# Seven half-size products for eight over the first four k tiles of ten gate and up pairs

## The chip, the cores and the metric

The program runs on one core of one Trainium2 chip. Its time is the device time of one execution in microseconds. Several executions were timed and one was profiled; the profile gives the span of the program on the core and, for each engine, every instruction's start and length. The engines are named as in the profile: PE (TensorE's matmuls), PEld (TensorE's weight loads), DVE (VectorE), ACT (ScalarE), POOL (GpSimd) and SP (which issues the weight DMAs; SPq is its queue).

## The reference

A block of a hybrid decoder: three token mixers, then a gated feed-forward network. The change lies in the latter, whose shapes are 256 tokens, D_MODEL = 2048 and D_FF = 5632, all in float32:

```python
x = x + rms_norm(h, norm_mix_post[l])
h = rms_norm(x, norm_ffn_pre[l])
h = swiglu(h, ffn_w_gate[l], ffn_w_up[l], ffn_w_down[l])
x = x + rms_norm(h, norm_ffn_post[l])

def swiglu(h, w_gate, w_up, w_down):
    return (jax.nn.silu(h @ w_gate) * (h @ w_up)) @ w_down
```

## The kernel before

**Products.** A float32 product is made of three matmuls in TensorE's fp32r form. Each operand is held as a high part (rounded to fp32r) and a low part (the rest), and high times high, high times low and low times high are summed in PSUM. The activations are split once, into `xh` and `xl`, with the channel on the partition: 16 k tiles of 128 channels by 256 tokens. A matmul's stationary operand is one k tile of 128 tokens (t = 0 or 1), its moving operand 512 columns of weights, its result a PSUM tile of 128 tokens by 512 columns.

**Weights.** `weights` streams them from DRAM. SP loads 1 MB at a time into a tile `raw` (four k tiles by 512 columns; `raw_bufs` is 3). Each half of `raw`, two k tiles or 128x1024, is split: ACT copies it into `wh` (L214), DVE subtracts that from `raw` into `wl` (L216). `wh` and `wl` have three buffers each (`h_bufs` is 3), so a split can begin when the matmuls of the third split before it are done. Twelve matmuls use each split: two k tiles, two token halves, three matmuls (L262 to L264 in `block_a_steps`).

**Gate and up.** The loop over j in `build` makes eleven pairs of 512 gate columns and 512 up columns. For j = 0 the two blocks alternate every four k tiles; for the others all 16 k tiles of gate come first, then all 16 of up. That is 2 blocks x 16 k tiles x 2 halves x 3 = 192 matmuls and 16 splits for one pair. The gate block has two PSUM tiles of tag `mm` and the up block two of tag `ptg`; each tag has three buffers. When a gate block is done, ACT applies silu (L1150) into `g`; when an up block is done, DVE multiplies (L1154). Then `split_channels` transposes `g` on PE (L285, four transposes for each token half), and ACT and DVE split the result into `ah` and `al` (L287, L288) for the last product, `w_down`.

**Order.** A scheduler puts the instructions of each engine in one fixed order when the program is built; an engine then runs its own list from first to last, and one that waits holds up all behind it. The gate and up weights are cast, subtracted and multiplied in the same order on ACT, DVE and PE.

Of the kernel before, what the change touches and what calls it, by code (L numbers as in the profile page):

```python
# [8 lines left out]
F32 = mybir.dt.float32  # L9
F32R = mybir.dt.float32r  # L10
AF = mybir.ActivationFunctionType
ALU = mybir.AluOpType
AX = mybir.AxisListType

P = 128
T = 256
D = 2048
KD = D // P
# [122 lines left out]
class Builder:  # L141
# [45 lines left out]
        return self.cst_t[:, o:o + n]  # L187


    def weights(self, wp, src, kts, width):  # L190

        nc, tc = self.nc, self.tc
        g = 2048 // width
        for k0 in range(0, kts, g):
            gk = min(g, kts - k0)
            raw = wp.tile([P, 2048], F32, name=self.uid("raw"), tag="raw", bufs=self.raw_bufs)
            ahead = FIRST if self.feeds else self.ahead
            rv = raw[:, :gk * width].rearrange("p (k c) -> p k c", c=width)
            n = gk // 2 if self.feeds else gk
            for i in range(0, gk, n):  # L200
                with tc.high_priority(ahead):
                    with tc.issue_after(self.load) if self.feeds and self.load else contextlib.nullcontext():
                        self.load = nc.sync.dma_start(rv[:, i:i + n], src[k0 // g][:, i:i + n]).ins
                    if self.feeds:
                        self.feeds.pop(0)()
            hg = 1024 // width
            for h0 in range(0, gk, hg):
                hk = min(hg, gk - h0)
                wh = wp.tile([P, 1024], F32R, name=self.uid("wh"), tag="wh", bufs=self.h_bufs)
                wl = wp.tile([P, 1024], F32R, name=self.uid("wl"), tag="wl", bufs=self.h_bufs)  # L210
                n = hk * width
                s = raw[:, h0 * width:h0 * width + n]
                with tc.high_priority(ahead):
                    nc.scalar.copy(wh[:, :n], s)  # L214
                with tc.high_priority(ahead), tc.issue_after(self.hold) if self.hold else contextlib.nullcontext():
                    nc.vector.tensor_tensor(wl[:, :n], s, wh[:, :n].bitcast(F32), ALU.subtract)  # L216
                hv = wh.rearrange("p (k c) -> p k c", c=width)
                lv = wl.rearrange("p (k c) -> p k c", c=width)
                for k in range(hk):
                    yield k0 + h0 + k, hv[:, k], lv[:, k]  # L220
# [657 lines left out]
def build(tc, aps, out):  # L878
    nc = tc.nc
    b = Builder(tc)  # L880
# [5 lines left out]
    pp = b.pp = b.pool("pp", space=bass.MemoryType.PSUM)  # L886
    b.dp = b.pool("dram", space=bass.MemoryType.DRAM)
    cp = b.pool("const")
    wp = b.pool("wp")
# [3 lines left out]
    def acts(s):  # L893
        return (xp.tile([P, KD, T], F32R, name=f"{s}h", tag="xh"), xp.tile([P, KD, T], F32R, name=f"{s}l", tag="xl"))
# [6 lines left out]
    xh, xl = acts("x")  # L901
# [66 lines left out]
    def direct(o, lead):  # L968

        t = b.slab(lead)  # L970
        cols(o, lambda ps: b.scaled(t[:, :, lead:lead + T], ps))
        return t
# [11 lines left out]
    def stage(s):  # L984
        return sp.tile([P, 512], F32, name=b.uid(s), tag="stage", bufs=b.stage_bufs)
# [16 lines left out]
    for q in range(4):  # L1002
        s = [direct(o + q, 1) for o in (BLK_RK, BLK_R, BLK_RV)]
# [5 lines left out]
        s = [direct(o + q, 3) for o in (BLK_Q, BLK_K, BLK_V)]  # L1009
# [15 lines left out]
    split = {}  # L1025
# [60 lines left out]
    x1 = []  # L1086
# [32 lines left out]
    xh, xl = acts("h")  # L1119
# [7 lines left out]
    with tc.high_priority(None), tc.issue_after(last):  # L1127
        rs = []
# [13 lines left out]
    ap_ = b.pool("ap")  # L1142
    ah = ap_.tile([P, KF, T], F32R, name="ah")
    al = ap_.tile([P, KF, T], F32R, name="al")
    for j in range(FF // 512):
        g = [stage("silu") for _ in range(2)]

        def gate(ps, g=g):
            for t in range(2):
                nc.scalar.activation(g[t], ps[t], AF.Silu, scale=rs[t])  # L1150

        def up(ps, g=g):
            for t in range(2):
                nc.vector.scalar_tensor_tensor(g[t], ps[t], rs[t], g[t], ALU.mult, ALU.mult)  # L1154

        steps = [b.block_a_steps(wp, pp, aps[w][j], xh, xl, KD, f) for w, f in (("w_gate", gate), ("w_up", up))]
        if j == 0:
            for _ in range(0, KD, 4):
                for st in steps:
                    for _ in range(4):  # L1160
                        next(st)
        for st in steps:
            for _ in st:
                pass
        b.hold = None
        for t in range(2):
            b.split_channels(pp, g[t], ah, al, 4 * j, t)

    x1 = []
    for t in range(2):  # L1170
        x1.append(ap_.tile([P, D], F32, name=f"x1r{t}"))
        nc.gpsimd.dma_start(x1[t], x1d[t])
    n4 = full(xp, "n4", aps["n4"], tag="xl")
    od = xp.tile([P, 2, D], F32, name="od", tag="xh")
# [9 lines left out]
    for t in range(2):  # L1184
        o = [od[:, t, j * 512:(j + 1) * 512] for j in range(4)]
        x = [x1[t][:, j * 512:(j + 1) * 512] for j in range(4)]
# [30 lines left out]
```

## Time and profile before

| what | value |
|---|---|
| time, median of 3 runs (lowest, highest) | 1848.22 us (1847.03, 1849.6) |
| time of the profiled execution | 1846.92 us |
| span of the profiled execution | 1845.1 us |
| granted TensorE clock over the span, as a share of full speed | 0.996 |
| busy PE, DVE, ACT | 1827.5, 1123.7, 863.8 us |

The profiled execution took 1.8 us more than its span; that part lies around the program. The span is the kernel's own work, and a change in a stage shows there one for one if the stage lies on the chain that ends last. A matmul's row gives its length from start to modelled end, and matmuls overlap, so what a matmul costs PE is the distance between two starts. The same goes, by a little, for DVE and ACT.

### The profile page before, as it was taken

What the parts mean: (1) busy time and instruction counts of PE and PEld (TensorE: products, weight loads), DVE (VectorE), ACT (ScalarE), POOL (GpSimd) and SP (SyncE); (2) the same over time, 40 slices, a digit from 0 to 9 for tenths busy, and PEclk for the clock granted to TensorE, in tenths of its full rate; (3) what the DMA queues carried; (4) which work ended last, traced back from release to release, by engine and by line L of the source; (5) the groups of instructions that cost most, each with busy time, mean ns of one, the idle gap of its engine ahead of it and who ended that gap; (6) DMA issues with size and microseconds to landing.
All of it is one profiled execution on the core that took longest, in us unless ns stands there. A gap on an engine that the chain in (4) does not pass through costs nothing.

```text
span 1845.1 us, 27756 instructions
## 1 busy us (share of the span) xinstructions
PE 1827.5 (99%) x11516; PEld 1578.7 (86%) x11516; DVE 1123.7 (61%) x1652; ACT 863.8 (47%) x1089; POOL 41.0 (2%) x76
## 2 busy tenths in 40 slices
PE   9999999999999999999999999999999999999998
PEld 9999997999899988887788878888888888888886
DVE  6768567866786677746665556555545445444444
ACT  7545345534553465444444446444444444443443
POOL 0000000000100010000000000000000000000000
PEclk9999999999999999999999999999999999999999
DMA  7545445444544454657765556555555555555553
GB/s 263 176 168 183 146 148 189 168 159 138 183 170 159 144 181 161 221 179 271 279 218 185 186 202 231 197 187 185 195 191 183 187 196 187 207 203 185 202 185 136
DMA packets 58574, 347.45 MB, mean 188 GB/s; under 512 B 6480, under 2 KB 7760, under 8 KB 19920
## 3 DMA queue, kind: packets, MB, share of 16 engines
q1 hardware_dynamic: 50832, 328.23, 50.8%
q10 hardware_dynamic: 7328, 15.36, 2.3%
q8 instruction: 90, 1.47, 0.3%
q0 software_dynamic: 288, 2.10, 0.3%
q14 instruction: 36, 0.29, 0.0%
HBM read 330.98 MB, written 14.68 MB: 187 GB/s over the span
## 4 chain that ended last, share of the span: by engine, by line
PE 96%; DVE 1%; ACT 1%; DMA 1%; issue 0%; POOL 0%; ACTq 0%; POOLq 0%; DVEq 0%; SPq 0%
PE mm L263 21%; PE mm L264 21%; PE mm L262 21%; PE mm L242 8%; PE mm L241 8%; PE mm L243 8%; PE tp L285 1%; PE px L568 1%; PE pr L603 1%; PE pr L592 1%; PE psa L599 1%; DMA raw<-in_w_branch_dram 1%; PE pst L609 0%; PE px L753 0%; PE px L482 0%
## 5 line engine op out<-in xcount | busy, mean ns | idle before, releaser
L216 DVE TENSOR_TENSOR wl<-raw,wh 128x1024 fp32r<-128x1024 f32 x590 | 721.4, 1224 | 607.0 <-ACT wh L214 604.4
L214 ACT CAST wh<-raw 128x1024 fp32r<-128x1024 f32 x590 | 620.5, 1052 | 839.3 <-PE mm L264 601.8
L242 PE MATMUL mm<-xl,wh 128*128 128x256 f32 x1200 | 342.5, 286 | 1.6 <-DVE xl L915 1.5
L241 PE MATMUL mm<-xh,wh 128*128 128x256 f32 x1200 | 342.8, 286 | 0.1
L243 PE MATMUL mm<-xh,wl 128*128 128x256 f32 x1200 | 341.4, 285 | 0.0
L264 PE MATMUL mm<-wh,hl 128*128 128x512 f32 x704 | 274.7, 390 | 0.0
L263 PE MATMUL mm<-wl,hh 128*128 128x512 f32 x704 | 274.6, 390 | 0.0
L262 PE MATMUL mm<-wh,hh 128*128 128x512 f32 x704 | 250.9, 392 | 2.0 <-ACT hh L311 2.0
L242 PEld LDWEIGHTS mm<-xl,wh 128*128 128x128 f32 x1200 | 229.8, 191 | 3.6 <-DVE xl L915 2.2
L241 PEld LDWEIGHTS mm<-xh,wh 128*128 128x128 f32 x1200 | 229.8, 191 | 1.9 <-ACT xh L914 0.5
L243 PEld LDWEIGHTS mm<-xh,wl 128*128 128x128 f32 x1200 | 229.5, 191 | 0.9 <-issue 0.3
L262 PEld LDWEIGHTS mm<-wh,hh 128*128 128x128 f32 x704 | 132.4, 188 | 29.6 <-ACT hh L311 2.6
L263 PEld LDWEIGHTS mm<-wl,hh 128*128 128x128 f32 x704 | 132.5, 188 | 27.6 <-DVE wl L216 0.4
L264 PEld LDWEIGHTS mm<-wh,hl 128*128 128x128 f32 x704 | 132.4, 188 | 27.5
L263 PE MATMUL mm<-wl,xh 128*128 128x512 f32 x384 | 151.7, 395 | 0.3 <-DVE wl L216 0.3
L264 PE MATMUL mm<-wh,xl 128*128 128x512 f32 x384 | 150.6, 392 | 0.0
L262 PE MATMUL mm<-wh,xh 128*128 128x512 f32 x384 | 141.3, 392 | 0.0
L264 PE MATMUL mm<-wh,al 128*128 128x512 f32 x352 | 136.9, 389 | 0.0
L263 PE MATMUL mm<-wl,ah 128*128 128x512 f32 x352 | 136.9, 389 | 0.0
L262 PE MATMUL mm<-wh,ah 128*128 128x512 f32 x352 | 123.6, 389 | 0.0
L263 PEld LDWEIGHTS mm<-wl,xh 128*128 128x128 f32 x384 | 72.1, 188 | 16.9 <-issue 1.0
L262 PEld LDWEIGHTS mm<-wh,xh 128*128 128x128 f32 x384 | 72.1, 188 | 16.0 <-issue 1.3
(297 smaller groups left out, 1951.4 us busy)
## 6 DMA issues: line engine op xcount, KB each, us to landing
raw<-in_w_in_dram SPq DMA_DIRECT2D x72, 1024.0 KB, 4.9
raw<-in_w_mix_dram SPq DMA_DIRECT2D x48, 1024.0 KB, 5.0
raw<-in_w_gate_dram SPq DMA_DIRECT2D x44, 1024.0 KB, 4.8
raw<-in_w_up_dram SPq DMA_DIRECT2D x44, 1024.0 KB, 4.9
raw<-in_w_down_dram SPq DMA_DIRECT2D x44, 1024.0 KB, 4.9
raw<-in_w_branch_dram SPq DMA_DIRECT2D x24, 1024.0 KB, 4.9
raw<-in_w_out_dram SPq DMA_DIRECT2D x16, 1024.0 KB, 4.8
keep<-stage ACTq DMA_DIRECT2D x28, 256.0 KB, 4.4
```

The costliest lines, as they stand in the source:

```text
L214: nc.scalar.copy(wh[:, :n], s)
L216: nc.vector.tensor_tensor(wl[:, :n], s, wh[:, :n].bitcast(F32), ALU.subtract)
L241: nc.tensor.matmul(o, hs, xh[:, k], start=(k == 0 and c == 0), stop=False, skip_group_check=True)
L242: nc.tensor.matmul(o, hs, xl[:, k], start=False, stop=False, skip_group_check=True)
L243: nc.tensor.matmul(o, ls, xh[:, k], start=False, stop=(k == kts - 1), skip_group_check=True)
L262: nc.tensor.matmul(ps[t], xh[:, k, ts], h, start=(k == 0), stop=False)
L263: nc.tensor.matmul(ps[t], xh[:, k, ts], l, start=False, stop=False)
L264: return nc.tensor.matmul(ps[t], xl[:, k, ts], h, start=False, stop=(k == kts - 1))
L285: nc.tensor.transpose(ps[:, k], src[:, k * P:(k + 1) * P], self.cst("id"))
L568: nc.tensor.matmul(ps[h][:, n * P:(n + 1) * P], bkc[hs, c, n], arc[hs, c, n], start=True, stop=True)
L592: nc.tensor.matmul(pq[bb, us], st[u][:, n, bb], sav[:, n, us], start=not n, stop=True, skip_group_check=True)
L599: nc.tensor.matmul(ps[bb, us], X[bb, 2 * u + p], R[bb, us], start=True, stop=True)
```

## The change

Only the pairs j = 1 to 10 change, and in them the first four of the 16 k tiles. These four k tiles (two blocks of two), the two token halves, and the two matrices gate and up make a product of 2x2 blocks by 2x2 blocks: token half by k block, times k block by matrix. Eight block products are replaced by seven (Strassen's algorithm in Winograd's form), each with a contraction over two k tiles.

- `sums` runs once, after pair 0. It adds and subtracts blocks of the activations on DVE and splits the four sums into `S`.
- `gate_up` replaces the two calls of `block_a_steps`. It loads the first `raw` of gate and of up together, makes four differences of weight blocks on DVE into `T` (128x1024 each; t1 and t2 first, then t4 and t3), and splits each of seven operands just before its product: b11, t1, t2, b21, t3, b22, t4.
- `product` has six matmuls for a split (two k tiles, three matmuls, one token half's worth of rows), where `block_a_steps` has twelve.
- The products are summed in four PSUM tiles: X takes four products, Y, Z and W one each. ACT copies X three times and Y once into tiles `m` while they are being filled (`keep`). The last two copies of X are called u2 and u3, the first one m1, that of Y m5.
- The other 12 k tiles go on in the old way, into Z and X for gate and W and Y for up. At their end DVE adds the kept copies (L1225, L1230; u2 gets m5 at L1216) before silu and the product with up.
- `T` and `S` lie in the buffers that the x1 tiles get after the loop.

```diff
+    def gate_up(j, S, g):
+        raw = []
+        for w in ("w_gate", "w_up"):
+            r = wp.tile([P, 2048], F32, name=b.uid("raw"), tag="raw", bufs=b.raw_bufs)
+            nc.sync.dma_start(r.rearrange("p (k c) -> p k c", c=512), aps[w][j][0])
+            raw.append([r[:, 0:1024], r[:, 1024:2048]])
+        (b11, b21), (b12, b22) = raw
...
+        def product(ps, a, w, start):
+            h, l = b.split(wp, w)
+            for k in range(2):
+                nc.tensor.matmul(ps, a[0][:, k], h[:, k], start=start and k == 0, stop=False, skip_group_check=True)
+                nc.tensor.matmul(ps, a[0][:, k], l[:, k], start=False, stop=False, skip_group_check=True)
+                nc.tensor.matmul(ps, a[1][:, k], h[:, k], start=False, stop=k == 1, skip_group_check=True)
...
+        product(X, act(0, 0), b11, True)
+        m1 = keep(X)
+        t1 = sub(0, b12, b11)
+        product(Y, s_(0), t1, True)
+        m5 = keep(Y)
+        t2 = sub(1, b22, t1)
+        product(X, s_(1), t2, False)
+        u2 = keep(X)
+        product(Z, act(0, 1), b21, True)
+        t4 = sub(0, b21, t2)
+        t3 = sub(1, b22, b12)
+        product(X, s_(2), t3, False)
+        u3 = keep(X)
+        product(W, s_(3), b22, True)
+        product(X, act(1, 1), t4, False)
+        nc.vector.tensor_tensor(u2, u2, m5, ALU.add)
+        for w, ps in (("w_gate", (Z, X)), ("w_up", (W, Y))):
+            for k, h, l in b.weights(wp, aps[w][j], KD, 512, first=4):
...
+            if w == "w_gate":
+                nc.vector.tensor_tensor(m1, Z, m1, ALU.add)
+                for t, src in ((1, X), (0, m1)):
+                    nc.scalar.activation(g[t], src, AF.Silu, scale=rs[t])
+            else:
+                for ps_, m, t in ((W, u2, 0), (Y, u3, 1)):
+                    nc.vector.tensor_tensor(m, ps_, m, ALU.add)
+                    nc.vector.scalar_tensor_tensor(g[t], m, rs[t], g[t], ALU.mult, ALU.mult)
```

What this does to the order is shown at the border between pairs 1 and 2; the other borders have the same order. On DVE before, from the last two splits of pair 1 to the first of pair 2 (numbers are buffers; `silu` is g):

```order
L216 TENSOR_TENSOR wl_11697<-raw_11694,wh_11696 128x1024
L216 TENSOR_TENSOR wl_11713<-raw_11694,wh_11712 128x1024
L1154 SCALAR_TENSOR_TENSOR silu_11394<-mm_11536,rstd_11074,silu_11394 128x512
L1154 SCALAR_TENSOR_TENSOR silu_11395<-mm_11537,rstd_11086,silu_11395 128x512
L216 TENSOR_TENSOR wl_11731<-raw_11728,wh_11730 128x1024
L216 TENSOR_TENSOR wl_11747<-raw_11728,wh_11746 128x1024
L288 TENSOR_TENSOR al<-tp_11676,ah 128x4x128
L288 TENSOR_TENSOR al<-tp_11683,ah 128x4x128
L216 TENSOR_TENSOR wl_11765<-raw_11762,wh_11764 128x1024
```

On DVE with the change, from the split of t1 on; ahead of it stand t1, t2 and the split of b11, and behind the last row the splits of b22 and t4 (mm_11413 and mm_11412 are W and Y of pair 1, m_11450 and m_11474 its u2 and u3):

```order
L195 TENSOR_TENSOR wl_11747<-T_11728,wh_11746 128x1024
L1230 TENSOR_TENSOR m_11450<-mm_11413,m_11450 128x512
L1185 TENSOR_TENSOR T_11728<-raw_11724,T_11728 128x1024
L1230 TENSOR_TENSOR m_11474<-mm_11412,m_11474 128x512
L1231 SCALAR_TENSOR_TENSOR silu_11403<-m_11450,rstd_11074,silu_11403 128x512
L195 TENSOR_TENSOR wl_11760<-T_11728,wh_11759 128x1024
L1231 SCALAR_TENSOR_TENSOR silu_11404<-m_11474,rstd_11086,silu_11404 128x512
L195 TENSOR_TENSOR wl_11772<-raw_11724,wh_11771 128x1024
L1185 TENSOR_TENSOR T_11728<-raw_11726 128x1024
L296 TENSOR_TENSOR al<-tp_11708,ah 128x4x128
L1216 TENSOR_TENSOR m_11769<-m_11769,m_11756 128x512
L296 TENSOR_TENSOR al<-tp_11715,ah 128x4x128
```

Between the split of t1 and that of t3 there are now eleven instructions, among them the end of pair 1 (two additions, two products, two `al`), and each split of pair 2 stands behind part of that.

On PE with the change, in the same place, after the six matmuls of b11 and of t1 (mm_11729 is X, mm_11730 Z, mm_11732 W; wh_11759 belongs to t2, wh_11771 to b21, wh_11783 to t3, wh_11795 to b22):

```order
L1191 MATMUL mm_11729<-wh_11759,S 128x512
L293 MATMUL tp_11708<-cst_t,silu_11403 128x128 x4
L1191 MATMUL mm_11730<-wh_11771,hh 128x512
L1192 MATMUL mm_11729<-wl_11760,S 128x512
...
L1192 MATMUL mm_11729<-wl_11760,S 128x512
L1193 MATMUL mm_11729<-wh_11759,S 128x512
L293 MATMUL tp_11715<-cst_t,silu_11404 128x128 x4
L1192 MATMUL mm_11730<-wl_11772,hh 128x512
...
L1193 MATMUL mm_11730<-wh_11771,hl 128x512
L1191 MATMUL mm_11729<-wh_11783,S 128x512
L1191 MATMUL mm_11732<-wh_11795,S 128x512
L1192 MATMUL mm_11729<-wl_11784,S 128x512
```

The eight transposes of pair 1, which stood together ahead of pair 2's third matmul, now stand in two fours among the products of t2 and b21. A product's first matmul needs only the cast part, and is put ahead of the five that need the subtracted part. On ACT the order of that stretch is: cast of t2, copy m1, cast of b21, copy m5, cast for `ah`, copy u2, cast for `ah`, casts of t3, b22 and t4, cast of the next gate half, copy u3.

## Rows read from the trace of the kernel before

**Rows 1.** The page's part on busy time: span, then engines

```profile
span 1845.1 us, 27756 instructions
PE 1827.5 (99%) x11516; PEld 1578.7 (86%) x11516; DVE 1123.7 (61%) x1652; ACT 863.8 (47%) x1089; POOL 41.0 (2%) x76
```

**Rows 2.** The page's chain of work that ended last, by engine

```profile
PE 96%; DVE 1%; ACT 1%; DMA 1%; issue 0%; POOL 0%; ACTq 0%; POOLq 0%; DVEq 0%; SPq 0%
```

**Rows 3.** Window of one pair: length, busy time by engine, clock, DMA

```profile
core 0: us, PE busy (x) PEld busy (x) DVE busy (x) ACT busy (x) POOL busy (x), PEclk, DMA share, GB/s
1245.36:1289.80 44.44, 44.44 (x202) 36.89 (x201) 22.24 (x21) 19.22 (x20) 0.00 (x0) 1.00 0.54 190
```

**Rows 4.** The chain from 1100 to 1610 us: start, length, what

```profile
1245.36 0.87 PE tp L285 x8
```

**Rows 5.** Timeline, PE before the border of 1245 us: start, length

```profile
1244.51 0.39 PE L262 MATMUL mm<-wh,hh 128*128 128x512 f32 x1
1244.74 0.39 PE L263 MATMUL mm<-wl,hh 128*128 128x512 f32 x1
```

**Rows 6.** Timeline, DVE at that border (in brackets: idle before, releaser)

```profile
1239.00 1.23 DVE L216 TENSOR_TENSOR wl<-raw,wh 128x1024 fp32r<-128x1024 f32 x1 [1.50 <-ACT wh L214]
1240.14 1.40 DVE L1154 SCALAR_TENSOR_TENSOR silu<-mm,rstd,silu 128x512 f32<-128x512 f32 x2
...
1244.44 1.23 DVE L216 TENSOR_TENSOR wl<-raw,wh 128x1024 fp32r<-128x1024 f32 x1 [1.49 <-ACT wh L214]
1246.45 1.29 DVE L288 TENSOR_TENSOR al<-tp,ah 128x512 fp32r<-128x512 f32 x2 [0.79 <-ACT ah L287]
1248.05 1.23 DVE L216 TENSOR_TENSOR wl<-raw,wh 128x1024 fp32r<-128x1024 f32 x1 [0.31 <-ACT wh L214]
```

**Rows 7.** Timeline, ACT at that border

```profile
1243.35 1.05 ACT L214 CAST wh<-raw 128x1024 fp32r<-128x1024 f32 x1 [1.66 <-PE mm L264]
1245.83 1.07 ACT L287 CAST ah<-tp 128x512 fp32r<-128x512 f32 x2 [1.43 <-PE tp L285]
```

**Rows 8.** Groups by line and shape: count, busy us, mean ns, idle before

```profile
L1154 DVE SCALAR_TENSOR_TENSOR silu<-mm,rstd,silu 128x512 f32<-128x512 f32 x22 | 15.4, 743 | 0.0
L288 DVE TENSOR_TENSOR al<-tp,ah 128x512 fp32r<-128x512 f32 x22 | 14.2, 686 | 8.7 <-ACT ah L287 8.7
L924 DVE TENSOR_TENSOR x<-x,x 128x1024 f32<-128x1024 f32 x3 | 3.7, 1218 | 0.0
L556 ACT COPY bkt<-px 128x512 f32<-128x512 f32 x8 | 4.4, 590 | 3.6 <-PE px L555 3.6
```

**Rows 9.** Timeline, DVE: splits that run without a pause between them

```profile
869.92 2.35 DVE L216 TENSOR_TENSOR wl<-raw,wh 128x1024 fp32r<-128x1024 f32 x2
1104.77 3.49 DVE L216 TENSOR_TENSOR wl<-raw,wh 128x1024 fp32r<-128x1024 f32 x3
```

**Rows 10.** Timeline, PE after a wait for ACT

```profile
1099.51 0.73 PE L262 MATMUL mm<-wh,hh 128*128 128x512 f32 x2 [1.54 <-ACT hh L311]
```

**Rows 11.** Windows before the first pair (columns as in rows 3)

```profile
1098.00:1100.00 2.00, 0.49 (x2) 0.30 (x2) 1.38 (x4) 2.00 (x7) 0.54 (x1) 1.00 0.30 127
1100.00:1102.00 2.00, 1.03 (x6) 0.43 (x4) 1.95 (x3) 0.51 (x3) 0.01 (x1) 0.81 0.94 397
1102.00:1104.00 2.00, 1.34 (x3) 0.62 (x4) 2.00 (x8) 0.87 (x4) 0.00 (x0) 0.50 0.23 94
1107.00:1108.00 1.00, 1.00 (x4) 0.74 (x3) 1.00 (x2) 0.21 (x1) 0.00 (x0) 0.50 0.00 0
```

**Rows 12.** Timeline, PE in the last of these stretches

```profile
1107.07 0.63 PE L263 MATMUL mm<-wl,hh 128*128 128x512 f32 x1
1107.49 0.63 PE L264 MATMUL mm<-wh,hl 128*128 128x512 f32 x1
```

**Rows 13.** DMA queue's own waits from 1156 to 1600 us; the page's issues

```profile
SPq L203 <- DVE wl L216: 411.6, 80, 5.9
raw<-in_w_gate_dram SPq DMA_DIRECT2D x44, 1024.0 KB, 4.8
```

More of the change, by code (lines that the diff above doesn't have):

```diff
@@ L187, in cst, with split, weights @@
         return self.cst_t[:, o:o + n]
-    def weights(self, wp, src, kts, width):
+    def split(self, wp, s):
+        h = wp.tile([P, 1024], F32R, name=self.uid("wh"), tag="wh", bufs=self.h_bufs)
+        l = wp.tile([P, 1024], F32R, name=self.uid("wl"), tag="wl", bufs=self.h_bufs)
+        self.nc.scalar.copy(h, s)
+        self.nc.vector.tensor_tensor(l, s, h.bitcast(F32), ALU.subtract)
+        return h.rearrange("p (k c) -> p k c", c=512), l.rearrange("p (k c) -> p k c", c=512)
+    def weights(self, wp, src, kts, width, first=0):
         nc, tc = self.nc, self.tc
         g = 2048 // width
-        for k0 in range(0, kts, g):
+        for k0 in range(first, kts, g):
             gk = min(g, kts - k0)
@@ L1144, in build, with sums @@
     al = ap_.tile([P, KF, T], F32R, name="al")
+    def sums():
+        t = ap_.tile([P, 2, D // 2], F32, name="sums", tag="x1r0")
+        x = t[:, 0].rearrange("p (k t) -> p k t", k=4)
+        o = t[:, 1].rearrange("p (i k t) -> p i k t", i=4, k=2)
+        nc.vector.tensor_tensor(x, xh[:, 0:4].bitcast(F32), xl[:, 0:4].bitcast(F32), ALU.add)
+        a = [[x[:, 2 * c:2 * c + 2, r * P:(r + 1) * P] for c in range(2)] for r in range(2)]
+        for i, (p, q, op) in enumerate(((a[1][0], a[1][1], ALU.add), (o[:, 0], a[0][0], ALU.subtract),
+                                        (a[0][0], a[1][0], ALU.subtract), (a[0][1], o[:, 1], ALU.subtract))):
+            nc.vector.tensor_tensor(o[:, i], p, q, op)
+        sp_ = ap_.tile([P, 2, 4, 2, P], F32R, name="S", tag="x1r1")
+        nc.scalar.copy(sp_[:, 0], o)
+        nc.vector.tensor_tensor(sp_[:, 1], o, sp_[:, 0].bitcast(F32), ALU.subtract)
+        return sp_
@@ new lines, in gate_up, with act, sub, keep @@
+    def gate_up(j, S, g):
[5 more added lines that the diff above has]
+        (b11, b21), (b12, b22) = raw
+        T = ap_.tile([P, 2, 1024], F32, name=b.uid("T"), tag="x1r0")
+        X, Z = [pp.tile([P, 512], F32, name=b.uid("mm"), tag="mm", bufs=b.mm_bufs) for _ in range(2)]
+        Y, W = [pp.tile([P, 512], F32, name=b.uid("mm"), tag="ptg", bufs=b.ps_bufs["ptg"]) for _ in range(2)]
+        def act(r, c):
+            return [m[:, 2 * c:2 * c + 2, r * P:(r + 1) * P] for m in (xh, xl)]
+        def sub(i, p, q):
+            nc.vector.tensor_tensor(T[:, i], p, q, ALU.subtract)
+            return T[:, i]
+        def product(ps, a, w, start):
[4 more added lines that the diff above has]
+                nc.tensor.matmul(ps, a[1][:, k], h[:, k], start=False, stop=k == 1, skip_group_check=True)
+        def keep(ps):
+            t = ap_.tile([P, 512], F32, name=b.uid("m"), tag="m", bufs=4)
+            nc.scalar.copy(t, ps)
+            return t
+        s_ = lambda i: (S[:, 0, i], S[:, 1, i])
+        product(X, act(0, 0), b11, True)
[16 more added lines that the diff above has]
+            for k, h, l in b.weights(wp, aps[w][j], KD, 512, first=4):
+                for t in range(2):
+                    ts = slice(t * P, (t + 1) * P)
+                    nc.tensor.matmul(ps[t], xh[:, k, ts], h, start=False, stop=False, skip_group_check=True)
+                    nc.tensor.matmul(ps[t], xh[:, k, ts], l, start=False, stop=False, skip_group_check=True)
+                    nc.tensor.matmul(ps[t], xl[:, k, ts], h, start=False, stop=k == KD - 1, skip_group_check=True)
+            if w == "w_gate":
[6 more added lines that the diff above has]
+                    nc.vector.scalar_tensor_tensor(g[t], m, rs[t], g[t], ALU.mult, ALU.mult)
@@ L1154, in up @@
                 nc.vector.scalar_tensor_tensor(g[t], ps[t], rs[t], g[t], ALU.mult, ALU.mult)
-        steps = [b.block_a_steps(wp, pp, aps[w][j], xh, xl, KD, f) for w, f in (("w_gate", gate), ("w_up", up))]
         if j == 0:
+            steps = [b.block_a_steps(wp, pp, aps[w][j], xh, xl, KD, f) for w, f in (("w_gate", gate), ("w_up", up))]
             for _ in range(0, KD, 4):
@@ L1161, in build @@
                         next(st)
-        for st in steps:
-            for _ in st:
-                pass
+            for st in steps:
+                for _ in st:
+                    pass
+            S = sums()
+        else:
+            gate_up(j, S, g)
         b.hold = None
@@ L1170, in build @@
     for t in range(2):
-        x1.append(ap_.tile([P, D], F32, name=f"x1r{t}"))
+        x1.append(ap_.tile([P, D], F32, name=f"x1r{t}", tag=f"x1r{t}"))
         nc.gpsimd.dma_start(x1[t], x1d[t])
```

## The prediction

> **What bounds the kernel now.** I read the busy times first: PE is busy for 99% of the span, DVE for 61%, ACT for 47% [rows 1]. The chain of work that ended last agrees: 96% of it lies on PE [rows 2]. In the stage of the change PE never waits: one pair takes 44.44 us, PE is busy in all of it at full clock, DVE in half, ACT in less than half [rows 3]. So a pair costs what its matmuls cost, and their price is the distance between two starts, not their length: 1244.51 to 1244.74 us, where each is 0.39 long [rows 5]. More exactly, the pair less the eight transposes' 0.87 us [rows 4] is 43.57 us for 192 matmuls, 0.227 each.
>
> What matters next is how far ahead of PE the other two engines are. A cast on ACT is let go by the last matmul of the split three before it, and the subtraction follows at once (idle 1.49 and 1.50, released by the cast [rows 6]; idle 1.66, released by PE [rows 7]). Nine matmuls of the new pair stand ahead of the transposes, so the pair's first one started at 1244.51 - 6 x 0.227 = 1243.15; the cast at 1243.35 was let go 0.20 behind it, and its subtraction began 1.09 after that, at 1244.44 [rows 5 to 7]. The lead is bounded by the three buffers, then, not by DVE's idle half.
>
> **What is removed.** Eight products of six matmuls become seven: 6 x 0.227 = 1.36 us for each of ten pairs, 13.6 us in all. The stretch of the seven products needs 42 x 0.227 + 0.87 = 10.40 us of PE, if it never waits.
>
> **What is added, and where.** For each pair DVE gets three more splits (1.23 each [rows 6]), four differences t1 to t4 (not in the trace in this form; an addition of the same size from SBUF takes 1.218 [rows 8]) and four additions of 128x512 (the nearest row with a PSUM input takes 0.686 [rows 8]): 3.7 + 4.9 + 2.7 = 11.3 us, which the 22.2 idle us of a pair would hide if it were spread. ACT gets three casts (1.05 each [rows 7]) and four copies out of PSUM (0.59 [rows 8]), 5.5 us on 25 idle. But the work falls into the seven products, where each split lasts PE only 6 x 0.227 = 1.36 us instead of 2.72, and where DVE also ends the pair before. There DVE is the slower one, and the three buffers let it start only 1.43 us ahead.
>
> The steps, with zero at the first matmul of b11: DVE instructions without a pause step by less than their length. Three splits take 3.49 us, so 1.13 each behind the first; two take 2.35 [rows 9]. Two `al` take 1.29, of which one is 0.69: a step of 0.60; two products with up take 1.40, of which one is 0.74: 0.66 [rows 6, 8]. I use 1.13, 0.60 and 0.66. The split of t1 uses the buffers of the last split but one of the old pair, which ends at -2.72; so its cast starts at -2.52 and its subtraction at -1.43. From there DVE runs its list without a pause: u2 + W at -0.30, t4 at 0.30, u3 + Y at 1.43, the two products with up at 2.03 and 3.82, the split of t2 between them at 2.69 (done 3.92), of b21 at 4.48 (done 5.71), t3 at 5.61 (done 6.83), `al`, u2 + m5 and `al` from 6.74 to 8.54, then the splits of t3 (done 9.77), b22 (10.90) and t4 (12.03).
>
> PE does b11 and t1 without a wait, to 2.72, then t2's first matmul, four transposes (0.43; their `g` is there at 2.77) and b21's first matmul, to 3.61. A released instruction starts about 0.05 late (cast at 1243.35, 1.05 long; subtraction at 1244.44 [rows 6, 7]). The waits:
> - for t2's subtraction until 3.97: 0.36 us; five matmuls and four transposes, to 5.54;
> - for b21's until 5.76: 0.22; five matmuls, to 6.90;
> - for the cast of t3, which starts only when DVE has made t3 at 6.83 and takes 1.05, until 7.98: 1.08; one matmul, to 8.21;
> - for the cast of b22, one cast later, until 8.91: 0.70; one matmul, to 9.13;
> - for t3's subtraction until 9.82: 0.69; five and five matmuls, to 12.09 (b22's subtraction is there at 10.90);
> - for u3's copy: X is free to copy at about 11.1, but ACT first casts the next gate half (1.05) and then copies (0.59), until 12.70. One matmul of that half runs meanwhile, so 0.38. Then t4's six.
>
> These are 3.43 us of waits. A matmul after a wait also costs a little more: two took 0.73 us behind a wait [rows 10], where 0.39 + 0.23 = 0.62 is usual. Most of that vanishes in the next wait; I add 0.2. A border thus costs 3.6 - 1.36 = 2.25 us. At the first of the ten borders pair 0 still ends in the old way, without two additions of 0.60, so 1.2 less. **The sum** is 10 x 2.25 - 1.2 = 21.3 us.
>
> A rule of the Trainium skill speaks for more. By its page VectorE: DVE Perf Modes, section The DRAIN you can't avoid, the next DVE operation does not start until the pipe of the one before is empty. Three splits in 3.49 us, each 1.23 long, show starts 0.1 us ahead of the recorded ends, so the trace does not bear that out for these forms.
>
> **What is hidden.** `sums` is 4 to 5 us of DVE (one addition at 1.22, four of a quarter the size, one split) in pair 0, whose 1.5 us of idle before each split [rows 6] cover it; uncovered, it costs at most that once. The loads: `raw` of gate and up is now held until about 5.7 and 10.9, so the gate load behind them is issued there instead of earlier. It lands 4.8 us later [rows 13], at 10.5; its cast is due when PE has done t4 and the third gate split is called for, about 14. Today SP itself waits for DVE, up to 5.9 us at a time [rows 13], without PE waiting. If that slack of 3.5 us were gone, each late us would cost 1 us for each pair. T and S hold back the x1 loads until the last pair is begun, over 200 us before x1 is used. Copies into `m` lie on ACT's idle half, but for u3's, counted above.
>
> **Rivals.**
> *PE does not wait, and the kernel is faster.* For it: DVE is idle half of the stage. The seven products would then save all 13.6 us: 1834.6. It needs t3's subtraction done by 6.9 instead of 9.8; it decides for "faster" once the waits of a border are below 1.36 us. Against it: the three 1.13 steps and five short ones between t1's and t3's splits can't start earlier, since W and Y of the old pair end at zero and the buffers come free in turn. I give 5% to faster, 3% to a tie.
> *The clock falls at each border.* Before the first pair PE was busy for only 0.49 of 2.00 us (1098 to 1100); the granted clock was 0.81 in the next 2 us, then 0.50, the 1.2 GHz level, until about 1108 [rows 11]. Matmuls then started 0.42 us apart [rows 12] instead of 0.227. With the change PE does only two matmuls between 6.90 and 9.82. If the clock fell there, the product of t4 alone would cost 6 x 0.19 = 1.2 us more, all 16 matmuls of the next 6.5 us 3.1; over ten borders 12 to 31 us: 1882 to 1901. Against it: the gap is cut in three, none over 1.1 us, and PE was idle for 1.54 at one go there [rows 10]. 17% for this at some or all borders.
> *DVE gains nothing from running without a pause.* Ten long, short and up-product steps of about 0.1 us more ahead of t3's split make 1.1 us for each border: 1881. Rows 9 speak against it; 4%.
> *The waits are shorter than worked out,* for example since ACT and DVE get one step ahead: with a third off, 3.43 becomes 2.3 and the change +10 us: 1858. 8%.
>
> **How the numbers follow.** The profiled execution took 1846.92 us and the median of the runs is 1848.22, 1.3 more. 1846.9 + 21.3 = 1868.2 for such an execution, 1869.5 for the median; I say 1870. This case, 1862 to 1877 us, has 63%. The range goes from 1859, into the shorter waits, to 1885, over DVE without gain and the clock falling at up to every border at its lower price: 63 + 4 + 5 + 9 = 81%. A measurement of this kernel can tell about 0.2%, 3.7 us, from no change. Slower 92%, same 3%, faster 5%.
>
> **What would show it.** In a pair's window PE should have 186 matmuls in some 46.7 us, no longer busy throughout; at each border the waits named above, longest that for the cast of t3, and DVE without a pause for some 13 us from 1.4 us before the border. DVE busy should rise by about 113 + 5 us to 1241, ACT's by 55. The prediction is wrong if PE shows no waits on L1191 and L1192, if DVE pauses within that stretch (then another chain rules), if the clock row leaves 1.00, or if waits for a `raw` load appear.

## The result, and the profile after

The changed kernel takes 1879.74 us (1877.25 to 1880.83), against 1847.38 (1846.72 to 1849.6) for the kernel before, timed beside it: 1.0172 times as long, 95% interval 1.0159 to 1.0185. That is 32 us slower, where 22 were forecast; it lies inside the forecast range.

The page of the changed kernel (span, busy times, chain by engine) answers to [rows 1, 2]:

```profile
span 1877.2 us, 27885 instructions
PE 1841.6 (98%) x11456; PEld 1574.8 (84%) x11456; DVE 1228.1 (65%) x1768; ACT 913.4 (49%) x1160; POOL 42.0 (2%) x76
PE 90%; DVE 7%; ACT 2%; issue 1%; DMA 0%; POOL 0%; ACTq 0%; POOLq 0%; DVEq 0%; SPq 0%
```

The span grew by 32.1 us. PE's busy time grew too, by 14.1, though it does 60 matmuls fewer: either a matmul's length grew or some ran at another clock. DVE, which had 1% of the chain, has 7%. PE's total still reads 98%; the loss has to be looked for in the stage.

Windows of the changed kernel; they answer to [rows 3]. The first and the last row are whole pairs (from b11's first matmul to that of the next pair), those between are single microseconds of the first one's border:

```profile
core 0: us, PE busy (x) PEld busy (x) DVE busy (x) ACT busy (x) POOL busy (x), PEclk, DMA share, GB/s
1245.64:1293.55 47.91, 46.09 (x195) 36.58 (x194) 32.30 (x32) 24.11 (x27) 0.00 (x0) 0.96 0.50 176
1255.00:1256.00 1.00, 0.65 (x2) 0.48 (x2) 1.00 (x2) 0.57 (x1) 0.00 (x0) 0.67 0.55 229
1256.00:1257.00 1.00, 1.00 (x4) 0.71 (x4) 1.00 (x2) 0.00 (x0) 0.00 (x0) 0.50 0.00 0
1257.00:1258.00 1.00, 1.00 (x4) 0.81 (x3) 0.74 (x1) 0.00 (x0) 0.00 (x0) 0.50 0.60 98
1258.00:1259.00 1.00, 1.00 (x5) 0.76 (x4) 0.00 (x0) 0.94 (x1) 0.00 (x0) 0.63 0.64 213
...
1293.55:1340.39 46.84, 45.02 (x195) 35.44 (x194) 32.29 (x32) 24.01 (x27) 0.00 (x0) 1.00 0.51 180
```

A pair of 44.44 us has become one of 47.91 or of 46.84. They have the same matmuls and differ by 1.07 us, in length and in PE's busy time; the granted clock is 0.96 in the first, 1.00 in the second. Within the first it falls to the 1.2 GHz level from about 1255.3 to 1258.7, and is full otherwise. Eight of the ten borders show this; the first (1152 us) and the one at 1293.55 don't.

PE's timeline at that border (in `product`, L1191 is the first matmul of a k tile and takes the cast part `wh`, L1192 takes the subtracted part `wl`):

```profile
1248.99 0.47 PE L1191 MATMUL mm<-wh,hh 128*128 128x512 f32 x1
1249.66 0.50 PE L1192 MATMUL mm<-wl,S 128*128 128x512 f32 x1 [0.19 <-DVE wl L195]
...
1252.49 0.40 PE L1193 MATMUL mm<-wh,hl 128*128 128x512 f32 x1
1253.72 0.50 PE L1191 MATMUL mm<-wh,S 128*128 128x512 f32 x1 [0.84 <-ACT wh L194]
1254.67 0.50 PE L1191 MATMUL mm<-wh,S 128*128 128x512 f32 x1 [0.45 <-ACT wh L194]
1255.52 0.79 PE L1192 MATMUL mm<-wl,S 128*128 128x512 f32 x1 [0.35 <-DVE wl L195]
1256.11 0.63 PE L1193 MATMUL mm<-wh,S 128*128 128x512 f32 x1
1256.54 0.63 PE L1191 MATMUL mm<-wh,S 128*128 128x512 f32 x1
...
1258.67 0.43 PE L1191 MATMUL mm<-wh,S 128*128 128x512 f32 x1
1258.95 0.40 PE L1192 MATMUL mm<-wl,S 128*128 128x512 f32 x1
...
1305.64 0.39 PE L1193 MATMUL mm<-wh,S 128*128 128x512 f32 x1
1306.01 0.50 PE L1221 MATMUL mm<-wh,hh 128*128 128x512 f32 x1
1306.50 0.50 PE L1191 MATMUL mm<-wh,hh 128*128 128x512 f32 x1
```

PE waits for t2's subtraction, the cast of t3, the cast of b22 and t3's subtraction. Between 1252.49 and 1255.52 it starts two matmuls. Then seven starts, until 1258.67, lie 0.43 apart, the pitch of [rows 12] (0.42) within the rounding. The last three rows are from the next border, whose clock held: there u3's copy holds up two starts, as the steps said. The brackets count idle time from a matmul's modelled end; a wait as the prediction counts it is the distance of two starts less 0.23.

DVE's timeline there, which answers to [rows 6]:

```profile
1244.25 1.23 DVE L195 TENSOR_TENSOR wl<-T,wh 128x1024 fp32r<-128x1024 f32 x1 [0.72 <-ACT wh L194]
1245.39 0.68 DVE L1230 TENSOR_TENSOR m<-mm,m 128x512 f32<-128x512 f32 x1
...
1251.32 1.22 DVE L1185 TENSOR_TENSOR T<-raw 128x1024 f32<-128x1024 f32 x1
...
1254.25 1.22 DVE L195 TENSOR_TENSOR wl<-T,wh 128x1024 fp32r<-128x1024 f32 x1
...
1256.52 1.22 DVE L195 TENSOR_TENSOR wl<-T,wh 128x1024 fp32r<-128x1024 f32 x1
```

Only the first row has idle time before it. From 1244.25 to 1257.74 DVE has no pause, and t3's split, started at 1254.25 and 1.22 long, ends at 1255.47; the matmul that needs it starts at 1255.52.

PE's waits in the changed kernel from 1190 to 1640 us, that is at nine borders (total, times, longest), then DVE's and ACT's groups there, which answer to [rows 8]:

```profile
PE mm L1191 <- ACT wh L194: 11.6, 18, 0.9
PE mm L1192 <- DVE wl L195: 4.8, 18, 0.4
```

```profile
L1185 DVE TENSOR_TENSOR T<-raw,T 128x1024 f32<-128x1024 f32 x18 | 22.0, 1220 | 0.3
L1231 DVE SCALAR_TENSOR_TENSOR silu<-m,rstd,silu 128x512 f32<-128x512 f32 x20 | 14.8, 744 | 0.0
L1230 DVE TENSOR_TENSOR m<-mm,m 128x512 f32<-128x512 f32 x20 | 13.6, 683 | 0.0
L1197 ACT COPY m<-mm 128x512 f32<-128x512 f32 x36 | 21.1, 586 | 13.8 <-PE mm L1193 13.8
```

No wait of PE for a load appears. SP now waits for DVE up to 11.0 us at a time, where it was 5.9 [rows 13].

### The profile page after: what moved, and what is told of

The parts are those of the page before. It is cut to its first block, busy times and chain, and to the rows that moved or that the text cites. A ratio compares the mean times of both kernels' runs of the same rounds, so it can differ in the third digit from the quotient of the medians.

```text
span 1877.2 us, 27885 instructions
## 1 busy us (share of the span) xinstructions
PE 1841.6 (98%) x11456; PEld 1574.8 (84%) x11456; DVE 1228.1 (65%) x1768; ACT 913.4 (49%) x1160; POOL 42.0 (2%) x76
## 4 chain that ended last, share of the span: by engine, by line
PE 90%; DVE 7%; ACT 2%; issue 1%; DMA 0%; POOL 0%; ACTq 0%; POOLq 0%; DVEq 0%; SPq 0%
PE mm L271 13%; PE mm L272 13%; PE mm L270 13%; PE mm L250 8%; PE mm L249 8%; PE mm L251 8%; PE mm L1221 5%; PE mm L1223 5%; PE mm L1222 5%; DVE wl L195 3%; DVE T L1185 1%; PE mm L1192 1%; PE mm L1193 1%; PE mm L1191 1%; DVE al L296 1%
## 5 line engine op out<-in xcount | busy, mean ns | idle before, releaser
L224 DVE TENSOR_TENSOR wl<-raw,wh 128x1024 fp32r<-128x1024 f32 x550 | 672.6, 1224 | 535.1 <-ACT wh L222 532.7
L222 ACT CAST wh<-raw 128x1024 fp32r<-128x1024 f32 x550 | 578.2, 1052 | 781.3 <-PE mm L272 372.9
L1222 PE MATMUL mm<-wl,hh 128*128 128x512 f32 x480 | 186.7, 389 | 0.0
L1223 PE MATMUL mm<-wh,hl 128*128 128x512 f32 x480 | 186.7, 389 | 0.0
L1221 PE MATMUL mm<-wh,hh 128*128 128x512 f32 x480 | 169.2, 390 | 0.0
L1221 PEld LDWEIGHTS mm<-wh,hh 128*128 128x128 f32 x480 | 90.4, 188 | 19.7 <-ACT wh L222 0.8
L1223 PEld LDWEIGHTS mm<-wh,hl 128*128 128x128 f32 x480 | 90.1, 188 | 18.8
L1222 PEld LDWEIGHTS mm<-wl,hh 128*128 128x128 f32 x480 | 90.1, 188 | 18.7
```

The costliest lines, as they stand in the source:

```text
L1221: nc.tensor.matmul(ps[t], xh[:, k, ts], h, start=False, stop=False, skip_group_check=True)
L1222: nc.tensor.matmul(ps[t], xh[:, k, ts], l, start=False, stop=False, skip_group_check=True)
L1223: nc.tensor.matmul(ps[t], xl[:, k, ts], h, start=False, stop=k == KD - 1, skip_group_check=True)
```

## The experiments

The theory: at each border DVE's list, which cannot start earlier and runs without a pause, makes PE wait (a net cost of 2.40 us a border, with the 1.36 saved already taken off), and those waits let the clock fall at eight borders (1.06 each). The rivals: the clock fall is only a companion of the slower pair and costs nothing of its own; or half-size products are slower for another reason (their pitch, or the loads).

**e1_filled** keeps PE at work in the largest wait: behind b21's product it does eight matmuls whose result is overwritten by W's own first product.

```diff
...
-        product(Z, act(0, 1), b21, True)
+        last = product(Z, act(0, 1), b21, True)
+        with tc.issue_after(last):
+            for _ in range(8):
+                nc.tensor.matmul(W, xh[:, 0, 0:P], xh[:, 0:2].rearrange("p k t -> p (k t)"), start=True, stop=True, skip_group_check=True)
```

> Eight extra matmuls into the still unused tile W stand on PE between the product of b21 and that of t3, where PE waits longest; their result is overwritten. Theory A (DVE's list at the border makes PE wait, and the wait lets the granted clock fall): no low clock at any of the ten borders, a border at 46.84 us from pair to pair as where it did not fall, so 8 x 1.06 = 8.5 us less than the change: 1871 (1868 to 1874). Theory B (the low clock has another cause than this wait, or costs nothing since PE waits anyway): 1879 to 1882, the eight matmuls being hidden or not.

Measured: 1870.18 us (1869.55 to 1871.39), 1.0128 [1.0114, 1.0141] of before. A pair's window, one of the same stretch as above, and PE's timeline:

```profile
1244.57:1291.41 46.84, 46.31 (x204) 36.93 (x202) 32.28 (x32) 24.02 (x27) 0.00 (x0) 1.00 0.52 180
1255.00:1256.00 1.00, 1.00 (x6) 0.75 (x5) 1.00 (x2) 0.09 (x1) 0.00 (x0) 1.00 0.04 16
```

```profile
1251.65 1.98 PE L1213 MATMUL mm<-hh 128*128 128x512 f32 x8
1253.46 0.65 PE L1191 MATMUL mm<-wh,S 128*128 128x512 f32 x2
1254.45 0.50 PE L1192 MATMUL mm<-wl,S 128*128 128x512 f32 x1 [0.34 <-DVE wl L195]
1254.78 0.39 PE L1193 MATMUL mm<-wh,S 128*128 128x512 f32 x1
```

More work, less time. Every border keeps its clock, every pair behind the first takes 46.8 us, and the span is 8.6 shorter than the changed kernel's: eight borders by 1.06. The matmul that waits for t3's subtraction starts 1254.45 - 1244.57 = 9.88 us after b11's first, and in the changed kernel 1255.52 - 1245.64 = 9.88: PE's filling moved DVE's list by nothing. So the clock's share is its own, and the rest is DVE's.

**e2_no_differences** leaves out the four weight differences (each product takes the first operand as it is).

```diff
...
         def sub(i, p, q):
-            nc.vector.tensor_tensor(T[:, i], p, q, ALU.subtract)
-            return T[:, i]
+            return p
```

> The four weight differences are left out: the products take b12, b22, b12 and b21 themselves, so the output is not the reference's. Theory A: DVE's list between the splits of t1 and t3 is 2.3 us shorter and the cast of t3 need not wait for DVE; the waits of a border fall from about 3.7 to 1.2 us and the clock holds: 1846 (1841 to 1855). Theory C (the half-size splits or ACT's extra casts and copies cost the time, not DVE's list): 1868 or more.

Measured: 1846.37 us, 0.9996 [0.9987, 1.0006]. All 42 product matmuls and seven splits are there, yet a pair takes 44.29 us. Of the waits one is left (nine borders):

```profile
PE mm L1219 <- ACT wh L222: 8.2, 9, 0.9
```

The half-size products are not slow in themselves. Four subtractions of DVE, 4.5 us, were worth 2.55 of a border's 46.84, and the clock's fall with it. A new last wait, the cast of the next gate half, keeps the rest of the 1.36.

**e3_no_additions** leaves out two of the four additions of kept copies (those ahead of the products with up).

```diff
-                    nc.vector.tensor_tensor(m, ps_, m, ALU.add)
-                    nc.vector.scalar_tensor_tensor(g[t], m, rs[t], g[t], ALU.mult, ALU.mult)
+                    nc.vector.scalar_tensor_tensor(g[t], ps_, rs[t], g[t], ALU.mult, ALU.mult)
```

> The two additions at the end of the up block (u2 + W, u3 + Y) are left out, the products with up read W and Y from PSUM as before the change; the output is not the reference's. Theory A: 1.2 us less for each of nine borders, and a shorter wait, so that the clock falls at fewer borders: 1858 (1856 to 1868). Theory C: these additions are hidden, 1878 to 1881.

Measured: 1860.44 us (1858.61 to 1860.93), 1.0072 [1.0058, 1.0086]. PE's waits at nine borders:

```profile
PE mm L1191 <- ACT wh L194: 8.4, 18, 0.5
PE mm L1192 <- DVE wl L195: 2.0, 9, 0.2
```

Two DVE instructions of 0.60 us a step made the pair 1.19 shorter (45.65), one for one, as when DVE's list sets the border. The clock stayed full at every border, with waits of half a microsecond.

**e4_spread** keeps all arithmetic of the change and only rearranges it: four splits of up's other k tiles, with twelve matmuls each, go between the half-size products, t4 is subtracted earlier, and b22's product goes ahead of t3's.

```diff
...
-        product(Y, s_(0), t1, True)
+        half(Y, s_(0), t1)
         m5 = keep(Y)
+        plain("up", 2)
         t2 = sub(1, b22, t1)
-        product(X, s_(1), t2, False)
+        half(X, s_(1), t2)
         u2 = keep(X)
-        product(Z, act(0, 1), b21, True)
         t4 = sub(0, b21, t2)
+        half(Z, act(0, 1), b21)
         t3 = sub(1, b22, b12)
-        product(X, s_(2), t3, False)
+        plain("up", 2)
+        half(W, s_(3), b22)
+        half(X, s_(2), t3)
         u3 = keep(X)
-        product(W, s_(3), b22, True)
-        product(X, act(1, 1), t4, False)
+        plain("up", 2)
+        half(X, act(1, 1), t4)
+        plain("up", 2)
...
```

Here `half` is `product`, and `plain(name, n)` does n of the old k tiles; the loop behind is left with what remains of them.

> The same seven products, with four classical splits of up (two k tiles each) put between them, after the products of t1, b21, t3 and t4, and t3 and t4 made earlier; all arithmetic is kept. Theory A: DVE and ACT get 2.72 us of PE time in between, the waits fall to about 0.3 us a pair, the clock holds, and most of the 13.6 us is saved: 1837 (1834 to 1843), faster than before the change. Theory C, or a limit in the totals of DVE: no faster than before, 1847 or more.

Measured: 1838.66 us (1838.24 to 1840.17), 0.9958 [0.9945, 0.997]: faster than both kernels, than the one before by 0.4%. A pair's window, and all waits of PE from 1190 to 1600 us:

```profile
1238.26:1281.80 43.54, 43.54 (x195) 35.57 (x194) 31.93 (x32) 23.93 (x27) 0.00 (x0) 1.00 0.54 194
```

```profile
PE tp L293 <- DVE silu L1249: 0.6, 1, 0.6
```

DVE has the same 32 us of work in a pair and PE no longer waits for its splits. Of the 1.36 us of matmuls 0.90 is kept (44.44 to 43.54); the rest goes in starts of 0.31 to 0.49 us around the first transposes and behind released matmuls, which the profile counts as busy.

**e5_copy_first** is e1_filled with ACT's copies of the PSUM tiles put ahead of the casts that are ready at the same time.

```diff
-            nc.scalar.copy(t, ps)
+            with tc.high_priority(FIRST):
+                nc.scalar.copy(t, ps)
```

> The kernel of e1 (gap filled, clock held), with ACT's copies out of X and Y put ahead of its other ready work, so that u3's copy no longer stands behind the cast of the next gate half. Theory A: the wait before t4's product falls by some 0.3 us at each border: 1867 (1865.5 to 1868.5) against 1870.2. Rival: that wait is hidden behind DVE's split of t4, 1869.5 to 1871.

Measured: 1867.58 us (1867.19 to 1867.99), 1.0109 [1.0095, 1.0123]. Pairs take 46.5 to 46.6 us, 0.3 less than in e1_filled: about the 0.38 that the steps gave to u3's copy.

**e6_pool_differences** moves the four differences to POOL.

```diff
-            nc.vector.tensor_tensor(T[:, i], p, q, ALU.subtract)
+            nc.gpsimd.tensor_tensor(T[:, i], p, q, ALU.subtract)
```

> The four weight differences are made by POOL instead of DVE, all arithmetic kept. No run here shows POOL on a 128x1024 subtraction. Theory A: DVE's list at the border is 2.3 us shorter as without the differences; if POOL makes one in about DVE's time, 1853 (1848 to 1858) and the clock holds; if POOL takes twice that or more, t3 and t4 come late and the gain goes: 1870 or above. Theory C (casts, copies and half-size splits cost the time): no change beside 1879.7.

Measured: 1895.74 us (1894.34 to 1900.41), 1.0259 [1.0245, 1.0273]. POOL's timeline at one border, then DVE's:

```profile
1247.85 3.26 POOL L1185 TENSOR_TENSOR T<-raw,T 128x1024 f32<-128x1024 f32 x1
1252.34 2.39 POOL L1185 TENSOR_TENSOR T<-raw,T 128x1024 f32<-128x1024 f32 x1 [1.23 <-DVE wl L195]
1257.22 3.24 POOL L1185 TENSOR_TENSOR T<-raw 128x1024 f32<-128x1024 f32 x1 [2.49 <-DVE wl L195]
```

```profile
1249.76 2.43 DVE L195 TENSOR_TENSOR wl<-T,wh 128x1024 fp32r<-128x1024 f32 x1 [0.91 <-ACT wh L194]
1252.12 1.28 DVE L1230 TENSOR_TENSOR m<-mm,m 128x512 f32<-128x512 f32 x2
1253.31 2.63 DVE L1231 SCALAR_TENSOR_TENSOR silu<-m,rstd,silu 128x512 f32<-128x512 f32 x2
...
1257.00 1.22 DVE L195 TENSOR_TENSOR wl<-raw,wh 128x1024 fp32r<-128x1024 f32 x1
1258.14 1.28 DVE L296 TENSOR_TENSOR al<-tp,ah 128x512 fp32r<-128x512 f32 x2
1259.34 1.68 DVE L1216 TENSOR_TENSOR m<-m,m 128x512 f32<-128x512 f32 x1
```

A difference takes POOL 2.4 to 3.3 us instead of 1.22, and what DVE does beside it grows. The split at 1249.76 ends 1.08 us after POOL's instruction that began first (1251.11), about its own length; the one at 1257.00 began ahead of POOL's and keeps its 1.22. The two `al` of 1258.14, which have one input in PSUM, keep their 1.28 beside POOL. The Trainium skill, SBUF — State Buffer, section Who interferes with whom, says that a VectorE instruction with two SBUF inputs contends with a GpSimd instruction that reads SBUF, that the port pair they share is an exclusive lock, and that the order of issue decides which one is blocked. These rows agree with it. PE's waits grew to pairs of 48.7 us, and to about 50 where the clock fell, which it did at nine borders.

**e7_spread_late_load** is e4_spread with t3 and t4 subtracted later and an up split between b22's and t4's products.

```diff
-        t4 = sub(0, b21, t2)
-        half(Z, act(0, 1), b21)
-        t3 = sub(1, b22, b12)
-        plain("up", 2)
-        half(W, s_(3), b22)
-        half(X, s_(2), t3)
-        u3 = keep(X)
-        plain("up", 2)
-        half(X, act(1, 1), t4)
-        plain("up", 2)
+        plain("up", 2)
+        half(Z, act(0, 1), b21)
+        t4 = sub(0, b21, t2)
+        t3 = sub(1, b22, b12)
+        half(X, s_(2), t3)
+        u3 = keep(X)
+        plain("up", 2)
+        half(W, s_(3), b22)
+        plain("up", 2)
+        half(X, act(1, 1), t4)
```

> The kernel of e4 with another order: the second pair of up k tiles stands before the product of b21, t3 and t4 are made after it, so that the weight tiles of gate and up are given back later and the third load of up is issued later. Theory A, with the three weight tiles as the next limit: a wait of 0.7 us for that load's cast and 0.4 us for a subtraction at each pair, 0.8 more than in e4: 1846 (1843 to 1848). Rival: the loads have slack, 1838 to 1840 as e4.

Measured: 1846.51 us (1844.53 to 1849.82), 0.9999 [0.9991, 1.0008]. The chain at the border with the longest wait, then PE's waits at nine borders:

```profile
1246.22 5.78 DMA raw<-in_w_up_dram
1252.11 1.05 ACT wh L222
1253.20 0.73 PE mm L1213 x2
```

```profile
PE mm L1213 <- ACT wh L222: 3.9, 9, 1.2
PE mm L1215 <- DVE wl L224: 0.8, 5, 0.2
```

The next up load is issued only when a `raw` tile comes free; freed later, it lands later, and PE waits for its cast. Spread work is not enough: the first two tiles must be given back early.

## Why the prediction was right in its sign and short in its size

**The matmuls saved, and DVE's timetable: right.** The starts at the border, counted from b11's first matmul (1245.64), are -1.39 for the split of t1, 5.68 for t3, 8.61 for its split and 10.88 for the split of t4; the steps said -1.43, 5.61, 8.54 and 10.80. The steps of 0.60 and 1.13 us and the absence of a pause hold, so the rival in which DVE gains nothing is out, and so is the one with shorter waits.

**The waits: right.** By distances of starts: t2's subtraction 0.44 (0.36 said), the cast of t3 1.00 (1.08), that of b22 0.72 (0.70), t3's subtraction 0.62 (0.69), u3's copy 0.14 + 0.26 = 0.40 where the clock held (0.38); that for b21's subtraction was about 0.1 (0.22). The starts right behind waits took some 0.11 more than the usual 0.23 at four places, 0.44 in all, where 0.2 was added. A border whose clock held costs 46.84 - 44.44 = 2.40 us, where 2.25 was said; part of the single differences cancels. e1_filled, e2_no_differences and e3_no_additions show by change of one thing that DVE's list sets it; that four subtractions are too many for this stretch is shown, not argued.

**The clock: this step failed.** The prediction had the fall as a rival at 17%, "Against it: the gap is cut in three, none over 1.1 us". Each wait was weighed by itself and the longest was compared with the 1.54 of [rows 10]. Together they left two matmuls between 1252.49 and 1255.52, and the clock fell at eight borders of ten; a clock row that leaves 1.00 was one of the prediction's own signs of being wrong. The fall came on top of the forecast case. Its price was 1.06 us, below the 1.2 to 3.1 that the prediction worked out: seven starts 0.2 us further apart make 1.4, but the 0.40 us of waiting for u3's copy vanishes behind them. e1_filled shows the price and that work in the gap prevents it. Why the border at 1293.55, with the same waits of 0.84, 0.45 and 0.35, kept its clock stays open. So does whether the three waits count together or the longest by itself: at the first border, where the waits were 0.55, 0.44 and 0.35, and in e3_no_additions, where none was over 0.5, both were smaller, and the clock held.

**The sum.** Of the span's 32.1 us, ten borders of 2.40, less 1.02 at the first, make 23.0 (21.3 was said); the clock makes 8 x 1.06 = 8.5; 0.6 lies elsewhere. Of it 0.24 is there before pair 0, whose first matmul starts at 1099.75 instead of 1099.51, and 0.09 is in pair 0, so that the next pair begins at 1151.92 instead of 1151.59; the rest was not traced. Without the clock the sum would have been met within 2 us: e1_filled is 23.3 us above the kernel before timed beside it (1870.18 against 1846.87). That its time meets the forecast of 1870 almost exactly is luck, since that figure was rounded up and stood on a slower median of before, 1848.22. That the measured 1879.74 lies in the range is owed to its upper part, which was kept for a fall of the clock.

**Smaller terms.** DVE's busy time rose by 104 us instead of 118, ACT's by 50 instead of 55: a pair's window shows 10.1 and 4.9 more, not 11.3 and 5.5. The work is as said: the lengths of all instructions, added up one by one, rose by 117 us on DVE and 56 on ACT. Busy time counts an overlap of two instructions once, and in a list without a pause each overlaps the next. The loads were hidden, as said, and `sums` lies in pair 0, which grew by 0.09 us. More buffers for the splits or for `raw`, which might let DVE start earlier, were not tried.

**Readings of before that were off.** No term of the sum rests on them. The matmul of 1243.15 opens the second split of the new pair and not its first: counted from pair 0's first matmul, 192 to a pair, the new pair begins at 1240.43, and the old pair's products with up, which need its sums, run from 1240.14 [rows 6]. So 21 matmuls of the new pair stand ahead of the transposes, neither nine nor two, and the first two splits in the order shown for DVE before are the new pair's: already then the old pair's end stood behind the new pair's second split. The lead is the same, since the casts at 1240.63 and at 1243.35 both start 0.20 us behind the first matmul of a split. Between the splits of t1 and t3 stand four long and seven short instructions, where one rival counts three and five and another makes ten steps of them.

## What to carry to other kernels

An engine that feeds the bottleneck has to be judged by its rate over the stretch in which the bottleneck eats fastest, with the lead that its buffers allow, and not by its busy share: DVE was half idle and still cost 23 us here. Work with a poor ratio of feeding to matmuls belongs between work with a good one (e4_spread), as long as the tiles that the loads need come free early. Several short waits close together can go with a fall of the clock, though each is shorter than a wait behind which it was seen to fall; so their shortness is no reason to say that the clock will hold.

## What the runs showed of the hardware that was not expected

Behind three waits of 0.35 to 0.84 us, with two matmuls between them, the clock fell to 1.2 GHz at eight of ten borders; each fall lasted 3.4 us (0.33 + 0.50 + 0.50 + 0.37 us of full clock are missing in the windows from 1255 to 1259, which at half clock is 3.4) and cost 1.06. Eight extra matmuls a border, 1.8 us of PE, made the span 8.6 us shorter. On POOL a subtraction of 128x1024 took at least 2.38 us (1.22 on DVE), and the DVE instructions with two SBUF inputs beside it took up to two and a half times as long (1.68 for the usual 0.68).
